# Low halves of 54 weight tiles by an adding DMA instead of VectorE, in a float32 decoder layer

## The chip, the cores and the metric

The kernel runs on one core of one Trainium2 chip. The metric is the device time of the whole program in microseconds, the median of several runs. A separate profiled execution gives the trace that is read here.

## The reference

One layer of a decoder trunk on 272 tokens (16 learned ones and 256 real), width 2048, all in float32: a half-step feed-forward network, a token mixer with two kinds of attention, and a second half-step feed-forward network. The change lies in the second half-step, which is computed for the 256 real tokens only:

```python
def _swiglu(x, w_gate, w_up, w_down):
    return (jax.nn.silu(x @ w_gate) * (x @ w_up)) @ w_down
...
h = h + FFN_RESIDUAL_WEIGHT * _swiglu(_rmsnorm(h, ffn2_norm[layer]), ffn2_w_gate[layer],
                                      ffn2_w_up[layer], ffn2_w_down[layer])
```

`w_gate` and `w_up` are 2048 x 5632, `w_down` is 5632 x 2048.

## The kernel before, in words

**Precision.** TensorE gets its factors as float32r. Each factor is split into a high part and a low part, and a product is three matmuls: high by high, high by low, low by high. For weights, ScalarE writes the high part `wh` (a copy from the float32 tile `raw` into a float32r tile), and VectorE then writes the low part `wl = raw - wh`.

**Units.** All weights go through TensorE in units of 512 KB (128 x 2 x 512), in the order of one list, `units`. For unit after unit the main loop calls `ahead(u)`, which loads (SP's DMA queue, into `raw`) and splits units that come later, and then `products(u)`. Loads run up to nine units ahead (`SECOND_AHEAD`), splits two (`SPLIT_AHEAD`). There are eight `raw` buffers in the second half-step, three of `wh` and three of `wl`. Inside each engine the instructions stay in the order that Tile's scheduler gives them; an engine that waits holds up all that stands behind it.

**The second half-step.** Its 11 column groups of 512 columns of gate and up are done in two ways. Nine (`SEVENS`) use a scheme of seven products instead of eight for each 2 x 2 block product: seven products `p1` to `p7`, each of four units with six matmuls, on sums and differences of weight blocks. The sums for p5, p6 and p7 were made in the first half-step and stored in DRAM (`sum`), p1 and p2 load parts of `w_gate`, p3 of `w_up`. p4 has no load: VectorE makes it in place from the raw tiles of p6 and p2. The order in a group is p1, p5, then p6, p2 and p4 by turns for each of the four units, then p3, p7. Between the units of the groups stand, one at a time, the plain units (12 matmuls each) of group 1 and of the down projection: one after each p2 unit, after every second unit of p5 and p3, and after the second unit of p1 and of p7. So a group is 28 units of six matmuls and ten plain ones.

In `split_unit` the copy of a group's unit is one line and its subtraction another (L1139 and L1145 in the profile; L1144 is the subtraction that makes p4). The plain units go through the helper `split` (L191 and L192). The matmuls of the groups are L1012, those of all other blocks L1213. Loads are issued at L1125 (groups) and L1130 (others). Evacuations of finished sums by ScalarE stand at L1019 (p1), L1022 (p5), L1033 (p4).

Other buffers: `slot` gives one of 25 buffers of 128 x 1024 float32 for values (tiles `v`), which also hold activations, sums and the evacuated results; `f` are the split activations.

Of the kernel before, what the change touches and what calls it, by code (L numbers as in the profile page):

```python
# [8 lines left out]
F32 = mybir.dt.float32  # L9
F32R = mybir.dt.float32r  # L10
AF = mybir.ActivationFunctionType
ALU = mybir.AluOpType
# [4 lines left out]
P = 128  # L17
# [15 lines left out]
SPLIT_BUFS = 3  # L33
LOAD_AHEAD = 6
SECOND_AHEAD = 9
SUMS_PACE = 0.94
SUMS_FROM = 20
PRE_BUFS = 9
# [14 lines left out]
def hybrid_layer(ctx: ExitStack, tc: tile.TileContext, x, meta_tokens, ffn1_norm, ffn1_w_gate, ffn1_w_up,  # L53
                 ffn1_w_down, mix_norm, w_in, b_forget, fox_q_norm, fox_k_norm, w_branch_fox, w_branch_sb,
                 w_out, ffn2_norm, ffn2_w_gate, ffn2_w_up, ffn2_w_down, out):
    nc = tc.nc
    act, dve, pe = nc.scalar, nc.vector, nc.tensor
# [13 lines left out]
    wp = ctx.enter_context(tc.tile_pool(name="weights", bufs=SPLIT_BUFS))  # L71
# [7 lines left out]
    def name(tag):  # L79
        uid[0] += 1  # L80
        return f"{tag}_{uid[0]}"

    def slot(shape, dt):
        return vp.tile(shape, dt, tag="v", name=name("v"))
# [105 lines left out]
    def split(hi, lo, src):  # L190
        act.activation(hi, src, AF.Copy)  # L191
        dve.tensor_tensor(lo, src, hi.bitcast(F32), op=ALU.subtract)  # L192
# [168 lines left out]
    def first_norm(c):  # L361

        ps = first_transposes(c)
        for i in range(2):
            first_parts(2 * c + i, ps[i])
        first_meta_parts(c)
        split_unit(c)
        first_residual(c, ps)
        for i in {1: (0, 1), 4: (4, 5), 5: (6,), 6: (7,), 7: ()}.get(c, (c,)):
            first_squares(i)  # L370
        if c == 2:
            meta_squares()
# [576 lines left out]
    def plain_group(g):  # L949

        u = {}
        factor = lambda i: norms["ffn2"].rtok[:, i:i + 1] if g == 0 else 1.0

        def ev_gate(i, ps):
            if i == 0:
                u["t"] = slot([P, 2, 512], F32)
            assert norms["ffn2"].done
            act.activation(u["t"][:, i, :], ps[:], AF.Silu, scale=factor(i))

        def ev_up(i, ps):  # L960
            s = u["t"][:, i, :]
            if g == 0:
                dve.scalar_tensor_tensor(s, ps[:], factor(i), s, op0=ALU.mult, op1=ALU.mult)
                free["g0"] = i == 1
            else:
                dve.tensor_tensor(s, ps[:], s, op=ALU.mult)
            if i == 1:
                lanes["turn"].append(turn(u["t"], hs2, 4 * g))

        def rhs(kt):  # L970
            if g == 0:
                return norms["ffn2"].rhs(kt)
            return [[forms[f"a{i + 1}{kt // 8 + 1}"][m][:, kt % 8, :] for i in range(2)] for m in range(2)]

        return [Block(w[0], 0, KT, g * 512, 512, rhs, NR, ev, True)
                for w, ev in ((ffn2_w_gate, ev_gate), (ffn2_w_up, ev_up))]
# [119 lines left out]
    def units_of(bs):  # L1096
        return [(b, k0, 1024 // b.cols) for b in bs for k0 in range(0, b.kts, 1024 // b.cols)]

    units = units_of(blocks)
# [5 lines left out]
    down = [down_blocks(t0, 4 * n, t0 + 4 * n == FT) for t0, n in zip(starts, PART)]  # L1105
    eight = [plain_group(1), *down]
    eight = [u for bs in eight for u in units_of(bs)]
    for g, p, u in seven:
        units.append((g, p, u))
        if p == "p2" or p in ("p5", "p3") and u % 2 or p in ("p1", "p7") and u == 1:  # L1110
            units.append(eight.pop(0))
    units += eight
    raws, halves, banks, newest = {}, {}, {}, []

    def raw_tile(shape):
        if loaded >= second and loaded % 8 >= RAW_BUFS:
            return ptile(shape, F32, "raw", 8 - RAW_BUFS)
        return wp.tile(shape, F32, tag="raw", name=name("raw"), bufs=RAW_BUFS)

    def load(u):  # L1120
        b, k0, n = units[u]
        if isinstance(b, Group):
            if k0 != "p4":
                t = raw_tile([P, 2, 512])
                nc.sync.dma_start(t[:], b.source(k0, n))  # L1125
                raws[u] = t
            return
        t = raw_tile([P, n, b.cols])
        rows = slice(b.row0 + k0 * P, b.row0 + (k0 + n) * P)
        q = nc.sync.dma_start(t[:], b.w[rows, b.col0:b.col0 + b.cols].rearrange("(k p) c -> p k c", p=P))  # L1130
        newest[:] = [q.ins]
        raws[u] = t

    def split_unit(u):
        b, k0, n = units[u]
        if isinstance(b, Group):
            wh, wl = (wp.tile([P, 2, 512], F32R, tag=t, name=name(t)) for t in ("wh", "wl"))
            raw = b.t.pop(k0) if k0 == "p4" else raws.pop(u)
            act.activation(wh[:], raw[:], AF.Copy)  # L1139
            if k0 == "p6":  # L1140
                b.t["p4"] = raw
            elif k0 == "p2":
                t = b.t["p4"]
                dve.tensor_tensor(t[:], t[:], raw[:], op=ALU.subtract)  # L1144
            dve.tensor_tensor(wl[:], raw[:], wh[:].bitcast(F32), op=ALU.subtract)  # L1145
            halves[u] = (wh, wl)
            return
        wh = wp.tile([P, n, b.cols], F32R, tag="wh", name=name("wh"))
        if b.stacked:
            raw, s = raws.pop(u), b.stacked  # L1150
            act.activation(wh[:], raw[:], AF.Copy)
            dve.tensor_tensor(wh[:, :, 32:32 + s], raw[:, :, :s], wh[:, :, :s].bitcast(F32), op=ALU.subtract)
            halves[u] = (wh, None)
            return
        wl = wp.tile([P, n, b.cols], F32R, tag="wl", name=name("wl"))
        split(wh[:], wl[:], raws.pop(u)[:])
        halves[u] = (wh, wl)
# [68 lines left out]
        if k0 + n == b.kts:  # L1226
            del banks[b]

    loaded = done = 0
    held = []  # L1230
    sums_due = 0.0

# [4 lines left out]
            yield 1  # L1237

    def ahead(u):
        nonlocal loaded, done, sums_due  # L1240
        if SUMS_FROM <= u < mixer - 2:
            sums_due += SUMS_PACE
            while sums_due >= 1:
                sums_due -= 1
                next(ahead_sums, None)
        while loaded < min(len(units), u + (LOAD_AHEAD if u < second else SECOND_AHEAD)):
            load(loaded)
            loaded += 1
        while done < min(len(units), u + 1 + SPLIT_AHEAD):
            split_unit(done)  # L1250
            done += 1
# [13 lines left out]
    for c in range(1, KT // 2):  # L1265
        with tc.issue_after(meta.ins):
            load_x(c)
            load(c)
    loaded = KT // 2
# [12 lines left out]
    done = KT // 2  # L1282
    start = KT // 2 - 1
    for u in range(start, len(units)):
        ahead(u)
        products(u)
# [33 lines left out]
```

## Time and profile before

| | |
|---|---|
| median of 3 runs | 2203.55 us (2202.67 to 2203.96) |
| profiled execution, its span | 2203.0 us, 34793 instructions |
| its own time outside the span | not listed apart; the span is 0.5 us under the median |
| granted TensorE clock, mean | 0.999 |
| DMA | 554.09 MB, mean 252 GB/s |
| GpSimd's DMA queue | 608 packets, 1.16 MB |

The profile names engines as PE (TensorE matmuls), PEld (its weight loads, which overlap), DVE (VectorE), ACT (ScalarE), POOL (GpSimd) and SP (the queue that issues most DMAs). `x<-y` says which tile is written from which. In square brackets, or after the bar, stands the idle time of the engine before an instruction and what ended it. The stage that the change touches lasts from about 1544 to 2148 us: nine groups.

### The profile page before, as it was taken

The numbers are of one execution on the slowest core, as the hardware profiler recorded it, in microseconds if no ns is written. First come the engines' busy times: TensorE is split into PE (matmuls) and PEld (weight loads), VectorE is DVE, ScalarE is ACT, GpSimd is POOL, SyncE is SP. The second block draws the span as 40 slices with busy tenths as digits, with TensorE's granted clock in tenths as the row PEclk, the third lists the DMA queues.
The fourth block names the chain that finished last, engine by engine and source line by source line (L and its number), as shares of the span: only waits on it lengthen the run. The fifth ranks groups of instructions, "written<-read, shape, count | busy, mean of one in ns | idle before, by whom it ended". The sixth has DMA issues, their size and how long they took to land.

```text
span 2203.0 us, 34793 instructions
## 1 busy us (share of the span) xinstructions
PE 2195.6 (100%) x13672; PEld 1992.5 (90%) x13672; DVE 1612.9 (73%) x1967; ACT 1174.5 (53%) x1475; POOL 52.5 (2%) x129
## 2 busy tenths in 40 slices
PE   9999999999999999999999999999999999999999
PEld 9999999999999999998899988888888888888887
DVE  6677666667766755889556776667888888888886
ACT  6344433334344454556435665458666666666663
POOL 0000000000000000110001100000000000000000
PEclk9999999999999999999999999999999999999999
DMA  7899999999999966555566556565788777888775
GB/s 226 275 335 330 334 319 345 338 347 334 341 339 339 327 201 191 168 162 164 183 191 171 145 153 200 182 188 164 240 269 271 263 257 263 273 273 268 261 256 173
DMA packets 262020, 554.09 MB, mean 252 GB/s; under 512 B 17288, under 2 KB 22240, under 8 KB 261856
## 3 DMA queue, kind: packets, MB, share of 16 engines
q1 hardware_dynamic: 259776, 548.34, 75.7%
q8 instruction: 107, 1.75, 0.3%
q10 hardware_dynamic: 1472, 2.37, 0.3%
q0 software_dynamic: 608, 1.16, 0.2%
q14 instruction: 57, 0.47, 0.1%
HBM read 493.07 MB, written 58.73 MB: 250 GB/s over the span
## 4 chain that ended last, share of the span: by engine, by line
PE 99%; DVE 0%; DMA 0%; ACT 0%; issue 0%; POOL 0%; SPq 0%; DVEq 0%; ACTq 0%; POOLq 0%
PE acc L1213 72%; PE acc L1012 16%; PE acc L1196 5%; PE acc L1199 3%; PE aux L729 1%; PE aux L602 1%; PE aux L442 1%; PE aux L700 0%; DMA v<-in_meta_tokens_dram 0%; PE aux L590 0%; PE acc L1174 0%; PE aux L875 0%; PE aux L340 0%; DVE wl L192 0%; PE aux L679 0%
## 5 line engine op out<-in xcount | busy, mean ns | idle before, releaser
L192 DVE TENSOR_TENSOR wl<-raw,wh 128x1024 fp32r<-128x1024 f32 (+1 forms) x609 | 743.7, 1222 | 420.4 <-ACT wh L191 416.7
L191 ACT ACTIVATE wh<-raw 128x1024 fp32r<-128x1024 f32 (+1 forms) x609 | 644.5, 1059 | 763.0 <-PE acc L1213 606.6
L1213 PE MATMUL acc<-v,wh 128*128 128x272 f32 x5264 | 991.6, 289 | 0.0
L1213 PEld LDWEIGHTS acc<-v,wh 128*128 128x128 f32 x5264 | 827.3, 189 | 0.4 <-ACT wh L191 0.2
L1213 PE MATMUL acc<-v,wl 128*128 128x272 f32 x2616 | 753.2, 289 | 0.6 <-DVE wl L192 0.6
L1213 PE MATMUL acc<-wh,v 128*128 128x512 f32 x1664 | 540.8, 392 | 0.0
L1213 PEld LDWEIGHTS acc<-v,wl 128*128 128x128 f32 x2616 | 490.8, 188 | 0.9 <-DVE wl L192 0.8
L1213 PEld LDWEIGHTS acc<-wh,v 128*128 128x128 f32 x1664 | 312.5, 188 | 64.4
L1145 DVE TENSOR_TENSOR wl<-raw,wh 128x1024 fp32r<-128x1024 f32 x252 | 305.1, 1222 | 41.6 <-ACT wh L1139 33.4
L1139 ACT ACTIVATE wh<-raw 128x1024 fp32r<-128x1024 f32 x252 | 266.5, 1060 | 124.1 <-PE acc L1213 74.0
L1213 PE MATMUL acc<-wl,v 128*128 128x512 f32 x832 | 327.8, 394 | 0.0
L1213 PEld LDWEIGHTS acc<-wl,v 128*128 128x128 f32 x832 | 156.2, 188 | 39.0 <-DVE wl L192 7.5
L1012 PE MATMUL acc<-wh,f 128*128 128x512 f32 x576 | 191.1, 393 | 0.0
L1196 PE MATMUL acc<-v,wh 128*128 128x512 f32 x512 | 160.5, 395 | 0.0
L1012 PE MATMUL acc<-wh,v 128*128 128x512 f32 x432 | 143.3, 389 | 0.0
L1012 PEld LDWEIGHTS acc<-wh,f 128*128 128x128 f32 x576 | 108.2, 188 | 22.5
L1199 PEld LDWEIGHTS acc<-v,wl 128*128 128x128 f32 x512 | 96.1, 188 | 21.9
L1012 PE MATMUL acc<-wl,f 128*128 128x512 f32 x288 | 113.2, 393 | 0.0
L1199 PE MATMUL acc<-v,wl 128*128 128x256 f32 x512 | 101.3, 279 | 0.0
L1012 PEld LDWEIGHTS acc<-wh,v 128*128 128x128 f32 x432 | 81.1, 188 | 16.9
L1012 PE MATMUL acc<-wl,v 128*128 128x512 f32 x216 | 84.0, 389 | 0.0
L1196 PEld LDWEIGHTS acc<-v,wh 128*128 128x128 f32 x512 | 78.4, 188 | 0.2
(267 smaller groups left out, 1392.6 us busy)
## 6 DMA issues: line engine op xcount, KB each, us to landing
raw<-in_ffn_w_down_dram SPq DMA_DIRECT2D x176, 512.0 KB, 5.4
raw<-in_ffn_w_gate_dram SPq DMA_DIRECT2D x175, 512.0 KB, 5.3
raw<-in_w_in_dram SPq DMA_DIRECT2D x162, 512.0 KB, 3.7
raw<-in_ffn_w_up_dram SPq DMA_DIRECT2D x140, 512.0 KB, 5.1
sum<-pre SPq DMA_DIRECT2D x108, 512.0 KB, 6.6
raw<-sum SPq DMA_DIRECT2D x108, 512.0 KB, 4.7
pre<-in_ffn_w_up_dram SPq DMA_DIRECT2D x72, 512.0 KB, 6.7
pre<-in_ffn_w_gate_dram SPq DMA_DIRECT2D x36, 512.0 KB, 6.9
```

The costliest lines, as they stand in the source:

```text
L191: act.activation(hi, src, AF.Copy)
L192: dve.tensor_tensor(lo, src, hi.bitcast(F32), op=ALU.subtract)
L442: pe.transpose(p[:, (2 * j + i) * P:(2 * j + i + 1) * P], u[:, i, c:c + P], ident[:])
L602: pe.matmul(po[:, :NR], a[:, ks], b[:, i * NR:(i + 1) * NR], start=n == 0, stop=n == 6)
L729: pe.matmul(o, a, b, start=start, stop=stop, skip_group_check=True)
L1012: pe.matmul(ps[:], a[:, kt, :], b[:, i, :], start=fresh and kt == 0 and m == 0, stop=kt == 7 and m == 2, skip_group_check=True)
L1139: act.activation(wh[:], raw[:], AF.Copy)
L1145: dve.tensor_tensor(wl[:], raw[:], wh[:].bitcast(F32), op=ALU.subtract)
L1196: pe.matmul(ps[:].rearrange("p (a t) -> p a t", a=2), wh[:, i, cs], x[:, :, :NR], start=k0 + i == 0, stop=False, skip_group_check=True)
L1199: pe.matmul(ps[:, :NR], wl[:, i, cs], x[:, 0, :NR], start=False, stop=k0 + i == b.kts - 1, skip_group_check=True)
L1213: pe.matmul(o, a, c, start=first and m == 0, stop=last and m == len(terms) - 1)
```

## The change

For the four p2 units of every group, and for the plain units behind the second unit of p1 and of p7 (six units in each of nine groups, 54 in all, the set `summed`), VectorE's subtraction is left out. In its place a new step `seed(u)`, up to five units ahead (`SEED_AHEAD`), takes a value buffer (`slot`), has ScalarE write the negated high part into it (a copy with scale -1 from `raw`), and has GpSimd issue a DMA that adds the same 512 KB of weights from DRAM to it. That tile is then the low part. The high part is copied from `raw` as before. So each of the 54 units is fetched from DRAM twice.

```diff
+SEED_AHEAD = 5
...
+    summed = set()
     for g, p, u in seven:
+        if p == "p2":
+            summed.add(len(units))
         units.append((g, p, u))
         if p == "p2" or p in ("p5", "p3") and u % 2 or p in ("p1", "p7") and u == 1:
+            if p in ("p1", "p7"):
+                summed.add(len(units))
             units.append(eight.pop(0))
...
+    def source_of(u):
+        b, k0, n = units[u]
+        if isinstance(b, Group):
+            return b.source(k0, n)
+        rows = slice(b.row0 + k0 * P, b.row0 + (k0 + n) * P)
+        return b.w[rows, b.col0:b.col0 + b.cols].rearrange("(k p) c -> p k c", p=P)
...
+    lows = {}
+
+    def seed(u):
+
+        t = slot([P, 2, 512], F32R)
+        act.activation(t[:], raws[u][:], AF.Copy, scale=-1.0)
+        nc.gpsimd.dma_start(t[:], source_of(u), accum_op=ALU.add)
+        lows[u] = t
...
-            wh, wl = (wp.tile([P, 2, 512], F32R, tag=t, name=name(t)) for t in ("wh", "wl"))
+            wh = wp.tile([P, 2, 512], F32R, tag="wh", name=name("wh"))
+            wl = lows.pop(u) if u in lows else wp.tile([P, 2, 512], F32R, tag="wl", name=name("wl"))
...
-            dve.tensor_tensor(wl[:], raw[:], wh[:].bitcast(F32), op=ALU.subtract)
+            if u not in summed:
+                dve.tensor_tensor(wl[:], raw[:], wh[:].bitcast(F32), op=ALU.subtract)
...
+        if u in lows:
+            act.activation(wh[:], raws.pop(u)[:], AF.Copy)
+            halves[u] = (wh, lows.pop(u))
+            return
...
+        while seeded < min(len(units), u + 1 + SEED_AHEAD):
+            if seeded in summed:
+                seed(seeded)
+            seeded += 1
         while done < min(len(units), u + 1 + SPLIT_AHEAD):
             split_unit(done)
             done += 1
```

ScalarE's list before, in group 5 (about 1764 to 1780 us), from the end of p1 through p5 to the first p2 unit. L191 writes plain units and transposed results (`v`), L1139 the groups' units; `wh_2915` is the high part of the first p2 unit, from `raw_2893`.

```order
L1139 ACTIVATE wh_2894_18613<-raw_2872_18520 128x1024
L1019 ACTIVATE v_2896_18623<-acc_2881_18554 128x512
L191 ACTIVATE v_2899_18631<-aux_2898_18626 128x2x256
L191 ACTIVATE wh_2901_18636<-raw_2875_18532 128x1024
L1139 ACTIVATE wh_2904_18647<-raw_2878_18548 128x1024
L1139 ACTIVATE wh_2907_18659<-raw_2882_18561 128x1024
L191 ACTIVATE wh_2910_18677<-raw_2885_18573 128x1024
L1139 ACTIVATE wh_2913_18689<-raw_2890_18599 128x1024
L1022 ACTIVATE v_2897_18624<-acc_2903_18640 128x512
L1139 ACTIVATE wh_2915_18700<-raw_2893_18611 128x1024
L191 ACTIVATE wh_2918_18719<-raw_2900_18634 128x1024
```

The same place of ScalarE's list after (L1139 is now L1161, the other lines are one further down); L1151 is the negated copy.

```order
L1161 ACTIVATE wh_2894_18632<-raw_2873_18541 128x1024
L1020 ACTIVATE v_2896_18642<-acc_2881_18573 128x512
L192 ACTIVATE v_2899_18650<-aux_2898_18645 128x2x256
L192 ACTIVATE wh_2901_18655<-raw_2876_18553 128x1024
L1161 ACTIVATE wh_2904_18666<-raw_2879_18569 128x1024
L1151 ACTIVATE v_2907_18678<-raw_2893_18630 128x1024
L1161 ACTIVATE wh_2908_18681<-raw_2882_18580 128x1024
L192 ACTIVATE wh_2911_18699<-raw_2885_18592 128x1024
L1161 ACTIVATE wh_2914_18711<-raw_2890_18618 128x1024
L1023 ACTIVATE v_2897_18643<-acc_2903_18659 128x512
L1161 ACTIVATE wh_2916_18722<-raw_2893_18630 128x1024
L1151 ACTIVATE v_2918_18739<-raw_2910_18697 128x1024
```

The negated copy of the first p2 unit (`raw_2893`) comes five rows ahead of its ordinary copy; the other rows keep their order.

GpSimd's list had nothing after the memset at the stage's start; now the 54 transfers follow it, these the first (`v` is the tile of the negated high part):

```order
L829 MEMSET shift_15166 128x48
L1152 DMA v_16806<-in_ffn_w_gate_dram 128x2x512
L1152 DMA v_16989<-in_ffn_w_gate_dram 128x2x512
L1152 DMA v_17050<-in_ffn_w_gate_dram 128x2x512
L1152 DMA v_17106<-in_ffn_w_gate_dram 128x2x512
L1152 DMA v_17160<-in_ffn_w_gate_dram 128x2x512
L1152 DMA v_17319<-in_ffn_w_up_dram 128x2x512
```

They stand in the order of the negated copies, one behind the other in GpSimd's queue. VectorE's list has 1954 rows before and 1900 after; SP's has 1053 in both.

More of the change, by code (lines that the diff above doesn't have):

```diff
@@ L1124, in load @@
                 t = raw_tile([P, 2, 512])
-                nc.sync.dma_start(t[:], b.source(k0, n))
+                nc.sync.dma_start(t[:], source_of(u))
                 raws[u] = t
@@ L1128, in load @@
         t = raw_tile([P, n, b.cols])
-        rows = slice(b.row0 + k0 * P, b.row0 + (k0 + n) * P)
-        q = nc.sync.dma_start(t[:], b.w[rows, b.col0:b.col0 + b.cols].rearrange("(k p) c -> p k c", p=P))
+        q = nc.sync.dma_start(t[:], source_of(u))
         newest[:] = [q.ins]
         raws[u] = t
+    lows = {}
[4 more added lines that the diff above has]
+        lows[u] = t
     def split_unit(u):
@@ L1227, in products @@
             del banks[b]
-    loaded = done = 0
+    loaded = seeded = done = 0
     held = []
@@ L1239, in ahead @@
     def ahead(u):
-        nonlocal loaded, done, sums_due
+        nonlocal loaded, seeded, done, sums_due
         if SUMS_FROM <= u < mixer - 2:
```

## The prediction

> **What bounds the kernel now.** I read the parts of the page on busy time and on the chain first, then cut the span into stages, then read the waits of TensorE, and the DMA last.
>
> ```profile
> PE 2195.6 (100%) x13672; PEld 1992.5 (90%) x13672; DVE 1612.9 (73%) x1967; ACT 1174.5 (53%) x1475; POOL 52.5 (2%) x129
> PE 99%; DVE 0%; DMA 0%; ACT 0%; issue 0%; POOL 0%; SPq 0%; DVEq 0%; ACTq 0%; POOLq 0%
> ```
>
> TensorE is busy for the whole span and 99% of the chain that ended last. So work taken off VectorE pays only where TensorE stands waiting for VectorE, and a new transfer costs only where TensorE comes to wait for it. All 54 changed units lie in the stage of the seven-product groups, which the view by windows cuts out (columns: window, its length, busy us and count of PE, PEld, DVE, ACT, POOL, then granted clock, DMA share, GB/s). The first half-step stands beside it, as the stage with the busiest DMA.
>
> ```profile
> 50.00:811.00 761.00, 760.43 (x6056) 760.17 (x6055) 509.88 (x587) 305.93 (x363) 5.50 (x18) 1.00 0.94 324
> 1544.00:2148.00 604.00, 604.00 (x2672) 491.12 (x2672) 518.93 (x493) 397.36 (x421) 0.00 (x0) 1.00 0.80 263
> ```
>
> In the 604 us VectorE is busy for 519 (86%), ScalarE for 397 (66%), GpSimd for nothing, and the 16 DMA engines for 0.80. What TensorE waits for there, from the view of waits of its weight loads from 1500 us on:
>
> ```profile
> PEld acc L1213 <- DVE wl L192: 9.1, 30, 0.4
> PEld acc L1012 <- DVE wl L1145: 1.3, 7, 0.2
> ```
>
> 37 waits, 10.4 us. Two kinds of them, from the timeline of the weight loads:
>
> ```profile
> 1761.32 0.19 PEld L1213 LDWEIGHTS acc<-wl,v 128*128 128x128 f32 x1 [0.18 <-DVE wl L192]
> 1770.18 0.19 PEld L1213 LDWEIGHTS acc<-wl,v 128*128 128x128 f32 x1 [0.40 <-DVE wl L192]
> ```
>
> And what they cost, from the chain in order of time (start, us, what):
>
> ```profile
> 1617.47 2.72 PE acc L1213 x12
> ...
> 1634.92 2.99 PE acc L1213 x12
> ```
>
> A plain unit of 12 matmuls takes 2.72 us, and 2.99 where the long wait (0.37 to 0.40) falls. The long wait stands in the plain units after p5 and p3, which the change leaves as they are; the one of 0.18 in the plain unit after p1, which it changes.
>
> **The change part by part.** The work that moves, from the groups by line of the 604 us (busy us, mean ns of one, idle before):
>
> ```profile
> L1145 DVE TENSOR_TENSOR wl<-raw,wh 128x1024 fp32r<-128x1024 f32 x248 | 300.2, 1222 | 41.2 <-ACT wh L1139 33.4
> L1139 ACT ACTIVATE wh<-raw 128x1024 fp32r<-128x1024 f32 x249 | 263.4, 1060 | 123.2 <-PE acc L1213 74.0 <-PE acc L1012 40.5 <-issue 6.7
> ```
>
> The nearest issue of GpSimd's, from the view of its source line (ns, least, median, most):
>
> ```profile
> L626 POOL DMA_DIRECT2D nck<-negc x8: 543/546/566, 849.0 to 1005.3; - x8
> ```
>
> VectorE loses 54 subtractions of 1.222 us, 66 us, and falls to 453 of 604. On the path that is worth the short waits in the changed units: eight of 0.18 after p1 and at most the seven of L1145, 2.7 us in all if each counted in full, and nothing where the 2.72 already holds them. I take 0. The long waits stay, because ScalarE is late there and not VectorE (its timeline, and one row of VectorE's):
>
> ```profile
> 1766.83 0.60 ACT L1019 ACTIVATE v<-acc 128x512 f32<-128x512 f32 x1 [0.28 <-PE acc L1012]
> 1767.32 0.59 ACT L191 ACTIVATE v<-aux 128x512 fp32r<-128x512 f32 x1
> 1767.80 1.06 ACT L191 ACTIVATE wh<-raw 128x1024 fp32r<-128x1024 f32 x1
> 1768.75 1.06 ACT L1139 ACTIVATE wh<-raw 128x1024 fp32r<-128x1024 f32 x1
> 1770.01 1.06 ACT L1139 ACTIVATE wh<-raw 128x1024 fp32r<-128x1024 f32 x1 [0.20 <-PE acc L1012]
> 1773.00 1.06 ACT L191 ACTIVATE wh<-raw 128x1024 fp32r<-128x1024 f32 x1 [1.93 <-PE acc L1213]
> ...
> 1776.22 1.05 ACT L1139 ACTIVATE wh<-raw 128x1024 fp32r<-128x1024 f32 x1
> ...
> 1768.90 1.22 DVE L192 TENSOR_TENSOR wl<-raw,wh 128x1024 fp32r<-128x1024 f32 x1 [0.26 <-ACT wh L191]
> ```
>
> VectorE stood idle for 0.26 us for the copy of 1767.80, which stood behind two evacuations that TensorE had just released; their order is unchanged.
>
> ScalarE gains 54 negated copies. Their form has no row; the copy of the same shape takes 1.060 us, so 57 us, and 455 of 604 (75%). At the place above the negated copy of the first p2 unit stands between the rows of 1768.75 and 1770.01. It runs from 1769.81 (the end of the former) to 1770.87 and moves the next copy by 0.86 us. The idle 1.93 us ahead of 1773.00 takes that up: cost 0. Behind a negated copy stand the ordinary copies and the evacuations in ScalarE's queue, and it waits for its weights to have landed, earlier than the ordinary copy did (SP's timeline, and the loads of the 604 us with their median time to landing):
>
> ```profile
> 1764.16 0.38 SPq L1125 DMA_DIRECT2D raw<-in_ffn_w_gate_dram  x1
> ...
> raw<-sum SPq DMA_DIRECT2D x108, 512.0 KB, 4.7
> raw<-in_ffn_w_down_dram SPq DMA_DIRECT2D x76, 512.0 KB, 5.0
> raw<-in_ffn_w_gate_dram SPq DMA_DIRECT2D x75, 512.0 KB, 5.1
> raw<-in_ffn_w_up_dram SPq DMA_DIRECT2D x44, 512.0 KB, 4.6
> ```
>
> This p2 unit was issued at 1764.16 and lands 5.1 us later, at 1769.3: 0.5 us before ScalarE comes to it. Before, its copy was the one at 1776.22, 7 us after the landing. So a lead of 7 us shrinks to about half a microsecond: no cost while loads land in 5 us, and a stall of ScalarE as soon as they take 6.
>
> GpSimd's queue is empty in this stage; 54 issues of about 0.55 us (the nearest row, for a quarter of the bytes) block nobody. SP's queue keeps its 1053 rows; the seeded plain units give their buffer back a subtraction earlier, which only starts loads earlier.
>
> The transfers are what remains. 263 GB/s over 604 us are 159 MB, the 303 loads of 512 KB above; 0.80 of 604 is 483 us of all 16 engines, so 1.595 us for each load, with 121 us free. The added transfer of 512 KB has no row. Its lower bound is one load, 54 x 1.595 = 86 us, which fits (569 of 604, 0.94). But its result is the tile's content plus the weights, so two operands of 512 KB come in for the 512 KB that go out, where a load has one in and one out. At twice a load it is 172 us, 51 us more than is free; as three transfers (a load, a fetch of the tile and a write) 258 us, 137 too many. I take twice, by its two operands. Once the engines are the bound, the stage lasts 655 us. The 7 us by which loads ran ahead are used up once, so the sum is 2203.0 + 51 - 7 = 2247 us, against the profiled execution's own span of 2203.0, 0.5 us under the median of the runs, 2203.55. For this case alone: if the engines move bytes as in the first half-step (324 / 0.94 = 345 GB/s), 215.5 MB take 625 us and the sum is 2217; if they cannot be kept busier than the 0.94 seen there, 655 / 0.94 = 697 and 2296.
>
> A rule of the Trainium skill bears on this price: its page "Collectives: The Full Stack", section "The bandwidth ceiling: the fold count and why AG ≠ RS ≠ AR", says that an adding transfer is slower for its two source reads and not for the addition, 62.28 against 32.35 GB/s, a factor of 1.93. By that the sum would be 2241; no run here shows it yet.
>
> What is late next, if so: the low half of a seeded unit at TensorE, or the loads at ScalarE, both behind full DMA engines.
>
> **Rivals.** *The transfer is hidden (same).* It costs one load, the share rises to 0.94, which the first half-step bears with TensorE busy for 760.4 of 761 us. It must also land in time. At the place above it can start at 1770.87, and TensorE loads that low half here:
>
> ```profile
> 1779.61 0.19 PEld L1012 LDWEIGHTS acc<-wl,f 128*128 128x128 f32 x1
> ```
>
> 8.7 us. The nearest landings are from 880 to 1100 us, where GpSimd also issues, and, for loads at a share of 0.94, from 50 to 811 us (the third row):
>
> ```profile
> raw<-in_w_in_dram SPq DMA_DIRECT2D x54, 512.0 KB, 3.7
> ...
> nck<-negc POOLq DMA_DIRECT2D x6, 136.0 KB, 3.8
> ...
> raw<-in_ffn_w_down_dram SPq DMA_DIRECT2D x88, 512.0 KB, 5.8
> ```
>
> Taking off the movement (1.6 and 0.4 us) leaves 2.1 and 3.4, so GpSimd's way costs 1.3 us more: 5.1 + 1.3 = 6.4 us, and 5.8 + 1.3 = 7.1 at 0.94, under 8.7. Time 2203, at most 2206. The Trainium skill's page "DMA: Bandwidth & Descriptors", section "Anatomy of one DMA — SWDGE (gpsimd) path", has 2.0 us plus the bytes at 436 GB/s, 3.2 us here, and so would side with this rival; the trace disagrees, since the 136 KB took 3.8 us where the rule has 2.3.
>
> *Hidden in bytes, late in time (slower).* The engines hold out, but a landing passes 8.7 us, or loads pass the 0.5 us that ScalarE has left, as the 5.8 just would. Each 0.7 us late at 54 places is 38 us, and about half, as the next transfer is under way meanwhile: 2222.
>
> *Three transfers.* 2203 + 137 - 7 = 2333.
>
> *VectorE's relief pays (faster).* If all 37 waits of TensorE went with VectorE's lower load, 10.4 us: 2193. It decides for faster once 4.4 us of them go; against it stands that ScalarE, not VectorE, ends the long ones.
>
> That the subtractions stay is no rival: VectorE's list is 54 rows shorter.
>
> **How the numbers follow.** Twice a load 0.48 (2217 to 2296), hidden 0.24, late in time 0.12, three transfers 0.10, relief 0.06. I predict the likeliest, 2247. The range from 2201 to 2300 leaves out the relief and the three transfers, 0.16. Within 0.2% (4.4 us) is about what a measurement of this kernel can tell from no change: faster 0.06, same 0.24, slower 0.70.
>
> **What would show it.** Right: in the stage a DMA share near 1.0, the new transfers landing after 9 us or more, loads after 6 or more, TensorE's weight loads waiting for the transfers or ScalarE's negated copies for raw tiles, and the stage longer than 604 us by 40 to 50. Wrong: a share of about 0.94 and landings of 6 to 7 us; then the second operand costs the engines nothing and the time stays. A stage longer at a share well below 1 would mean that landing time, not bytes, decides.

## The result, and the profile after

The changed kernel takes 2258.98 us in the median (2255.01 to 2260.18) against 2203.69 for the kernel before on the same chip: a ratio of 1.0249 (95% interval 1.0237 to 1.0262), 55 us slower. Its profiled execution has a span of 2256.9 us. The two lines of its page on busy time and on the chain:

```profile
PE 2212.7 (98%) x13672; PEld 1990.1 (88%) x13672; DVE 1550.2 (69%) x1913; ACT 1219.7 (54%) x1529; POOL 119.2 (5%) x183
PE 70%; issue 25%; DMA 2%; POOL 2%; DVE 1%; ACT 0%; POOLq 0%; SPq 0%; DVEq 0%; ACTq 0%
```

VectorE has its 63 us less and ScalarE its 45 us more in the whole span, but TensorE is no longer the whole chain. (The 25% of "issue" is time for which the profile shows no releaser; the waits below tell more.) The view by windows, same columns as before, shows where the time went:

```profile
1544.00:2201.00 657.00, 620.83 (x2664) 489.41 (x2663) 454.86 (x438) 442.06 (x474) 65.11 (x54) 0.99 0.94 284
2201.00:2257.00 56.00, 51.13 (x228) 41.59 (x227) 36.66 (x44) 21.47 (x22) 0.00 (x0) 1.00 0.53 174
```

The stage of the groups takes 657 us instead of 604 for the same matmuls (2664 and 2672 in the records), what follows it 56 instead of 55. So the loss is all in the stage. The DMA share is 0.94, not 1. The waits of TensorE's weight loads there (us in total, times, longest):

```profile
PEld acc L1240 <- DVE wl L193: 16.9, 31, 1.1
PEld acc L1013 <- DMA v<-in_ffn_w_gate_dram: 14.6, 14, 2.2
PEld acc L1013 <- DVE wl L1168: 13.3, 15, 1.1
PEld acc L1013 <- ACT wh L1161: 7.4, 10, 1.9
PEld acc L1240 <- DMA v<-in_ffn_w_down_dram: 7.0, 6, 1.9
PEld acc L1240 <- ACT wh L192: 6.7, 6, 1.6
```

With two rows of 1.0 us that is 68 us, where the kernel before had 10. There are two kinds. Some 24 us are waits for the adding transfers (`v<-`). The other 44 are waits for ScalarE's high parts and for VectorE's low parts. What holds ScalarE up, from its own waits:

```profile
ACT v L1151 <- DMA raw<-in_ffn_w_gate_dram: 28.7, 17, 3.7
ACT v L1151 <- DMA raw<-in_ffn_w_down_dram: 25.2, 11, 4.0
```

The negated copies (L1151) wait 57 us in all for raw tiles that have not landed; in the kernel before ScalarE waited for no load in this stage. The timeline shows one such wait going through to TensorE (issue of a load, three rows of ScalarE, a weight load of TensorE):

```profile
1803.47 0.37 SPq L1138 DMA_DIRECT2D raw<-in_ffn_w_gate_dram  x1
...
1805.60 1.06 ACT L1161 ACTIVATE wh<-raw 128x1024 fp32r<-128x1024 f32 x1 [0.34 <-PE acc L1013]
1809.97 1.06 ACT L1151 ACTIVATE v<-raw 128x1024 fp32r<-128x1024 f32 x1 [3.31 <-DMA raw<-in_ffn_w_gate_dram]
1810.94 1.04 ACT L1161 ACTIVATE wh<-raw 128x1024 fp32r<-128x1024 f32 x1
...
1812.03 0.19 PEld L1013 LDWEIGHTS acc<-wh,f 128*128 128x128 f32 x1 [1.47 <-ACT wh L1161]
```

ScalarE starts on the tile of a load issued at 1803.47 only 6.5 us later. It stands idle for 3.31 us in front of the negated copy of that tile, the next high part comes late, and TensorE waits 1.47 us for it. The DMA rows of the stage (queue: packets, MB, share of 16 engines; then count, size, median us to landing):

```profile
q1 hardware_dynamic: 68363, 158.44, 68.8%
q0 software_dynamic: 14416, 27.79, 24.6%
...
raw<-sum SPq DMA_DIRECT2D x107, 512.0 KB, 5.4
...
raw<-in_ffn_w_gate_dram SPq DMA_DIRECT2D x75, 512.0 KB, 6.4
...
v<-in_ffn_w_gate_dram POOLq DMA_DIRECT2D x37, 512.0 KB, 8.9
v<-in_ffn_w_down_dram POOLq DMA_DIRECT2D x15, 512.0 KB, 8.4
```

By their MB there are 302 loads and 53 recorded transfers of 512 KB. 68.8% of 657 us is 452, 1.50 us of all 16 engines for a load; 24.6% is 162, 3.05 for an adding transfer: twice a load. Loads land in 5.4 to 6.6 us (4.6 to 5.1 before), the two larger groups of transfers in 8.4 and 8.9.

The profile leaves three theories open. *Bytes:* the engines cannot carry loads and transfers in 604 us. *Late:* the transfers land after TensorE needs them. *Held:* ScalarE, whose queue is in order, is held up by loads that the negated copies ask for early. The experiments take them apart. In the first expectations SCALARE stands for a cost of the 54 extra copies on ScalarE itself; HELD comes in with the later ones.

### The profile page after: what moved, and what is told of

Same layout as the page of the kernel before. It is cut to its first block, busy times and chain, and to the rows that moved or that the text cites. A ratio compares the mean times of both kernels' runs of the same rounds, so it can differ in the third digit from the quotient of the medians.

```text
span 2256.9 us, 34969 instructions
## 1 busy us (share of the span) xinstructions
PE 2212.7 (98%) x13672; PEld 1990.1 (88%) x13672; DVE 1550.2 (69%) x1913; ACT 1219.7 (54%) x1529; POOL 119.2 (5%) x183
## 4 chain that ended last, share of the span: by engine, by line
PE 70%; issue 25%; DMA 2%; POOL 2%; DVE 1%; ACT 0%; POOLq 0%; SPq 0%; DVEq 0%; ACTq 0%
PE acc L1240 58%; PE acc L1223 5%; PE acc L1226 3%; POOL v L1152 2%; DMA v<-in_ffn_w_down_dram 1%; PE acc L1013 1%; PE aux L730 1%; PE aux L603 1%; DMA v<-in_ffn_w_gate_dram 0%; DMA raw<-in_ffn_w_gate_dram 0%; DVE wl L193 0%; PE aux L443 0%; PE aux L701 0%; PE aux L591 0%; DMA v<-in_meta_tokens_dram 0%
## 5 line engine op out<-in xcount | busy, mean ns | idle before, releaser
L193 DVE TENSOR_TENSOR wl<-raw,wh 128x1024 fp32r<-128x1024 f32 (+1 forms) x591 | 722.1, 1223 | 474.7 <-ACT wh L192 472.9
L192 ACT ACTIVATE wh<-raw 128x1024 fp32r<-128x1024 f32 (+1 forms) x591 | 625.1, 1058 | 717.5 <-PE acc L1240 586.7
L1240 PEld LDWEIGHTS acc<-v,wh 128*128 128x128 f32 x5264 | 827.4, 189 | 0.4 <-ACT wh L192 0.2
L1168 DVE TENSOR_TENSOR wl<-raw,wh 128x1024 fp32r<-128x1024 f32 x216 | 260.3, 1222 | 102.8 <-ACT wh L1161 99.3
L1161 ACT ACTIVATE wh<-raw 128x1024 fp32r<-128x1024 f32 x252 | 262.7, 1055 | 106.3 <-PE acc L1013 41.4
L1240 PE MATMUL acc<-wl,v 128*128 128x512 f32 x766 | 303.4, 396 | 5.2 <-DVE wl L193 5.2
L1240 PEld LDWEIGHTS acc<-wl,v 128*128 128x128 f32 x766 | 144.5, 189 | 43.0 <-DVE wl L193 14.5
L1013 PE MATMUL acc<-wl,v 128*128 128x512 f32 x216 | 85.5, 396 | 6.7 <-DVE wl L1168 6.6
L1151 ACT ACTIVATE v<-raw 128x1024 fp32r<-128x1024 f32 x54 | 56.8, 1056 | 57.4 <-DMA raw<-in_ffn_w_gate_dram 28.7
L1013 PE MATMUL acc<-wl,f 128*128 128x512 f32 x216 | 84.4, 391 | 1.4 <-DVE wl L1168 1.4
```

The costliest lines, as they stand in the source:

```text
L1013: pe.matmul(ps[:], a[:, kt, :], b[:, i, :], start=fresh and kt == 0 and m == 0, stop=kt == 7 and m == 2, skip_group_check=True)
L1151: act.activation(t[:], raws[u][:], AF.Copy, scale=-1.0)
L1240: pe.matmul(o, a, c, start=first and m == 0, stop=last and m == len(terms) - 1)
```

## The experiments

All times are medians beside the kernel before on the same chip. For orientation, all of them in one table, with sums from the profiled executions: the DMA share from 1544 to 2148 us, all waits of TensorE's weight loads from 1544 us on, those of them for the transfers, and ScalarE's waits for raw tiles. In plain_copy, no_transfer, near_source, high_source, high_ahead7 and high_none the low parts hold other values than the product needs; these kernels serve for their times alone.

| kernel | us | over before | DMA share | TensorE's waits | of them for transfers | ScalarE's for raw |
|---|---|---|---|---|---|---|
| before | 2203.7 | | 0.80 | 10 | | 0 |
| high_none | 2206.1 | +2 | 0.80 | 13 | | 0 |
| high_ahead7 | 2206.7 | +3 | 0.99 | 14 | 1 | 3 |
| high_unread | 2208.9 | +6 | 0.99 | 17 | | 0 |
| no_transfer | 2212.5 | +8 | 0.79 | 18 | | 21 |
| only18 | 2227.5 | +23 | 0.83 | 36 | 9 | 33 |
| plain_copy | 2227.7 | +24 | 0.90 | 40 | 1 | 40 |
| high_source | 2247.6 | +44 | 0.94 | 55 | 45 | 0 |
| raw9 | 2253.0 | +50 | 0.94 | 59 | 23 | 62 |
| after | 2259.0 | +55 | 0.94 | 70 | 25 | 57 |
| near_source | 2267.5 | +64 | 0.92 | 67 | 12 | 59 |
| ahead3 | 2269.6 | +66 | 0.92 | 75 | 28 | 63 |
| unread | 2272.3 | +68 | 0.93 | 67 | | 68 |
| near_unread | 2274.2 | +71 | 0.91 | 75 | | 72 |

**1. One operand instead of two (plain_copy).**

```diff
-        nc.gpsimd.dma_start(t[:], source_of(u), accum_op=ALU.add)
+        nc.gpsimd.dma_start(t[:], source_of(u))
```

> The 54 transfers overwrite the tile instead of adding to it (the low part is then the weights themselves; the negated copies, queues and waits stay as in the changed kernel), so one operand comes in where two did. Theory BYTES (the second operand costs the DMA engines as much as a load, demand 452+162 us and more): a transfer takes about 1.5 us of 16 engines instead of 2.99, the stage's DMA share falls to about 0.90 or the stage gets shorter at the same share, loads land in about 5 to 6 us, time 2203 to 2215. Theory LATE (the way through GpSimd's queue and its landing time of 8.9 us cost the time, not the engines): the landing falls by 1.5 us at most, time 2235 to 2255. Theory SCALARE (54 more copies on ScalarE cost it): unchanged, 2255 to 2260.

2227.69 us, ratio 1.0103 (1.0088 to 1.0118). The DMA rows, from 1544 to 2195 us:

```profile
q1 hardware_dynamic: 71660, 164.80, 74.6%
q0 software_dynamic: 14688, 28.32, 15.0%
...
v<-in_ffn_w_gate_dram POOLq DMA_DIRECT2D x37, 512.0 KB, 6.0
```

15.0% of 651 us over 54 transfers is 1.81 us each, against 3.05 with the addition; landing falls from 8.9 to 6.0 us. TensorE waits for hardly any transfer (1 us), yet 24 us are lost at a share of 0.90. None of the three expectations fits alone: the engines are not full, and TensorE does not wait for the transfers, but ScalarE still waits 40 us for raw tiles.

**2. No transfer at all (no_transfer).**

```diff
-        nc.gpsimd.dma_start(t[:], source_of(u), accum_op=ALU.add)
```

> The negated copies stay, the 54 transfers are left out altogether (the low part is then minus the high part; nothing is fetched twice), VectorE's subtractions stay left out. All that is left of the change is 57 us more on ScalarE and 66 us less on VectorE. Theories BYTES and LATE: 2203 to 2206, TensorE's waits in the stage near the 10 us of the kernel before. Theory SCALARE: 2230 to 2260. Theory RELIEF (VectorE's lower load would pay if nothing else were in the way): 2193 to 2199.

2212.45 us, 1.0036 (1.0022 to 1.0051), between the expectations. The share is that of the kernel before, and still 8 us are lost. ScalarE's waits:

```profile
ACT v L1151 <- DMA raw<-in_ffn_w_down_dram: 13.8, 12, 3.0
ACT v L1151 <- DMA raw<-in_ffn_w_gate_dram: 6.0, 13, 0.8
```

Even with loads landing as fast as before, some negated copies come before their tile. ScalarE's list is the same row for row here, in plain_copy and in the changed kernel; its waits for raw tiles are 21, 40 and 57 us, and the loads from `w_gate` land in 5.0, 5.7 and 6.4 us. So the transfers cost time in this way by making the loads land later. No gain from VectorE's relief shows.

**3. Transfers that nobody reads (unread).** VectorE subtracts all low parts again, TensorE reads those; seeds and transfers are made.

```diff
-            wl = lows.pop(u) if u in lows else wp.tile([P, 2, 512], F32R, tag="wl", name=name("wl"))
+            wl = wp.tile([P, 2, 512], F32R, tag="wl", name=name("wl"))
+            lows.pop(u, None)
...
-            if u not in summed:
+            if True:
...
-        if u in lows:
-            act.activation(wh[:], raws.pop(u)[:], AF.Copy)
-            halves[u] = (wh, lows.pop(u))
-            return
+        lows.pop(u, None)
```

> Negated copies and adding transfers are all made, but VectorE subtracts as in the kernel before and TensorE reads that low part: nobody waits for what the 54 transfers bring, apart from the reuse of their buffers. Theory BYTES: the engines carry the same load, so loads are late and ScalarE waits for them, time 2240 to 2258, share 0.93 to 0.95. Theory LATE (TensorE waits for the landing of the low tiles): 2203 to 2215. A time halfway, near 2230, would mean that the loss is made of both about equally, as TensorE's new waits behind transfers (25 us) and behind ScalarE and VectorE (the rest) suggest.

2272.26 us, 1.0321 (1.0298 to 1.0345): slower than the change itself, though no wait for a transfer can be left. TensorE's waits:

```profile
PEld acc L1013 <- ACT wh L1162: 21.5, 13, 3.1
PEld acc L1013 <- DVE wl L1169: 19.7, 22, 1.6
PEld acc L1238 <- ACT wh L192: 13.5, 6, 4.2
PEld acc L1238 <- DVE wl L193: 12.2, 31, 1.1
```

They are all behind ScalarE, which waits 68 us for raw tiles, or behind VectorE, which works on ScalarE's results. So the late landings at TensorE are not the only route. Bytes or Held remain.

**4. Only the 18 plain units (only18).**

```diff
-        if p == "p2":
-            summed.add(len(units))
```

> Only the 18 plain units (behind the second unit of p1 and of p7) get their low part by an adding transfer, the 36 p2 units are subtracted by VectorE as before. Theory BYTES: 18 x 2.99 = 54 us on top of the 483 us of the 303 loads, 537 of 604 us, a share of 0.89, below what the stage bore: 2203 to 2208. Theory LATE: the loss goes by the number of transfers, 18 of 54 of the 55 us: 2218 to 2225. Theory SCALARE: the same third, 2218 to 2225.

2227.46 us, 1.0107 (1.0092 to 1.0122), just above the 2218 to 2225 that LATE and SCALARE expected. The window of the stage:

```profile
1544.00:2148.00 604.00, 588.90 (x2581) 473.09 (x2580) 481.07 (x459) 398.11 (x423) 20.50 (x17) 1.00 0.83 270
```

A third of the transfers at a share of 0.83, with engine time left over, lose 42% of the whole. That speaks against Bytes.

**5. and 6. The negated copy from another raw tile (near_source), and that with unread tiles (near_unread).**

```diff
-        act.activation(t[:], raws[u][:], AF.Copy, scale=-1.0)
+        act.activation(t[:], raws[min(raws)][:], AF.Copy, scale=-1.0)
```

> The negated copy reads the raw tile that is split next instead of the one five units ahead (so the low parts hold wrong values; the DMA still adds the weights of the right unit). ScalarE's work, the 54 adding transfers, their queue and TensorE's reading of them stay; the only thing gone is that ScalarE stands still behind a load that has not landed (57 us of it in the changed kernel). Theory HELD (the loss comes through ScalarE, held up by loads that the negated copy asks for too early): its waits for raw fall under 5 us, time 2203 to 2222. Theory BYTES (the engines cannot carry 452 + 162 = 614 us in 604): share stays at 0.94 to 0.97 and loads stay late, 2240 to 2258. Theory LATE (landing at TensorE): no change in its waits for the tiles, 25 us, time 2225 to 2235.

> As the run before, and besides VectorE subtracts all low parts as in the kernel before and TensorE reads those: nobody waits for a seeded tile, and ScalarE does not wait for early loads. What is left of the change is the 54 adding transfers on the DMA engines and 57 us of ScalarE. Theory HELD: 2203 to 2215. Theory BYTES: 2240 to 2260. Against the run before it gives what TensorE's waits for the tiles cost: theory LATE puts this run at 2203 to 2210 and the one before 20 or more above it.

2267.47 us (1.0287, 1.026 to 1.0315) and 2274.19 (1.0322, 1.0307 to 1.0337). They lie even above what Bytes expected, but the edit did not do what it was for. ScalarE's waits in near_source:

```profile
ACT v L1151 <- DMA raw<-in_ffn_w_down_dram: 33.8, 16, 3.9
ACT v L1151 <- DMA raw<-sum: 14.7, 7, 3.5
```

With two smaller rows 59 us, where the changed kernel has 57. The scheduler moved 32 of the 54 copies forward in ScalarE's list, by 1 to 9 rows, now that their tile was an earlier one, and there they stood in front of loads again. These two runs tell nothing of the theories, save that the place on ScalarE is the scheduler's choice.

**7. Seeds three units ahead (ahead3).**

```diff
-SEED_AHEAD = 5
+SEED_AHEAD = 3
```

> Seeds go three units ahead instead of five: the negated copy comes about two units (3.4 us) later, so loads have that much more time, and the adding transfer has that much less until TensorE wants the tile (about 5.3 us where it lands in 7 to 9). Theory HELD: ScalarE's waits for raw fall under 10 us, but TensorE then waits 2 to 3 us for most of the 54 tiles, partly covered by each other: 2250 to 2300, its waits now put down to the transfers and not to ScalarE. Theory BYTES: the same demand, 2250 to 2260, waits split as before.

2269.63 us, 1.0295 (1.0278 to 1.0313). ScalarE's waits for raw tiles stayed at 63 us, since the constant hardly moved anything: in ScalarE's list 53 of the 54 negated copies stand in the same row as in the changed kernel. The first one moved five rows back, to two rows ahead of its unit's ordinary copy, and TensorE's longest wait for a transfer became 7.0 us. The run tells nothing of the trade between the two leads.

**8. and 9. The negated copy from a tile that needs no load (high_source), and that with unread tiles (high_unread).** The copy now reads the high part that ScalarE has just written, so it cannot come to stand in front of a load. Against the changed kernel 22 of the 54 copies stand one to four rows later in ScalarE's list, and none earlier.

```diff
-        act.activation(t[:], raws[u][:], AF.Copy, scale=-1.0)
+        act.activation(t[:], halves[done - 1][0][:].bitcast(F32), AF.Copy, scale=-1.0)
```

> The negated copy reads the high part that ScalarE has just written for another unit, so it stands in the same place of ScalarE's list as in the changed kernel (within a row or two) but waits for no load at all (the low parts hold wrong values; ScalarE's work, the 54 adding transfers and TensorE's reading of them stay). This is what near_source was meant to be; there the scheduler moved the copies forward until they waited for loads again (59 us). Theory HELD (the loss is ScalarE standing in its queue behind loads that have not landed): waits for raw under 5 us, time 2203 to 2222. Theory BYTES (614 us of transfers do not fit into 604 us, nor more than a share of 0.94): 2240 to 2260, with the waits for raw tiles now at the high parts' copies. Theory LATE (landing of the low tiles at TensorE): waits for v tiles of 25 us stay and are most of what is left, 2225 to 2235.

> The same, and VectorE subtracts all low parts as in the kernel before and TensorE reads those. What is left of the change is 57 us of ScalarE and the 54 adding transfers' load on the DMA engines, with nobody waiting for them. Theory HELD: 2203 to 2212. Theory BYTES: 2240 to 2270. Theory LATE: 2203 to 2210 here, and the run before 20 us above it.

2247.62 us (1.0205, 1.0188 to 1.0223) and 2208.92 (1.0024, 1.0015 to 1.0033). The stage of high_unread, and its two large queues in these 604 us:

```profile
1544.00:2148.00 604.00, 603.02 (x2651) 486.35 (x2650) 512.82 (x488) 444.28 (x471) 63.84 (x53) 1.00 0.99 307
```

```profile
q1 hardware_dynamic: 67969, 157.18, 73.1%
q0 software_dynamic: 14416, 27.79, 25.8%
```

The loads of the kernel before in its 604 us:

```profile
q1 hardware_dynamic: 68459, 158.59, 79.7%
```

This settles Bytes. The engines carry 300 loads and 53 adding transfers in 604 us, at a share of 0.99, while TensorE is busy for 603 of them. 441 us go to the loads, 1.47 each (481 us before, 1.59 each), and 156 to the transfers, 2.94 each. With nobody waiting for either, the full traffic and ScalarE's 57 us cost 6 us. Between unread (+68) and high_unread (+6) only the source of the negated copy differs, with it the place of some copies in the list, and ScalarE's 68 us of waits for raw tiles are gone: theory Held is shown as one route. The other route is in TensorE's waits in high_source:

```profile
PEld acc L1013 <- DMA v<-in_ffn_w_gate_dram: 23.5, 24, 2.2
PEld acc L1240 <- DMA v<-in_ffn_w_down_dram: 17.1, 15, 1.9
PEld acc L1240 <- DVE wl L193: 10.6, 30, 0.4
```

With two smaller rows there are 42 waits for transfers, 45 us, 1.06 us each, and the waits behind ScalarE are gone. Between high_source (+44) and high_unread (+6) TensorE's reading of the transferred tiles and VectorE's share of the work differ: theory Late. Held alone had put high_source at 2203 to 2222, and Late at 2225 to 2235; both were too low. The time lies in the range of Bytes, 2240 to 2260, but not for its reason: Bytes had put high_unread at 2240 or more.

**10. Nine raw buffers (raw9).**

```diff
-SECOND_AHEAD = 9
-V_BUFS = 25
+SECOND_AHEAD = 10
+V_BUFS = 24
...
-        if loaded >= second and loaded % 8 >= RAW_BUFS:
-            return ptile(shape, F32, "raw", 8 - RAW_BUFS)
+        if loaded >= second and loaded % 9 >= RAW_BUFS:
+            return ptile(shape, F32, "raw", 9 - RAW_BUFS)
```

> The changed kernel whole, with nine raw buffers instead of eight in the second half-step and loads ten units ahead, paid for with one of the 25 value buffers: each load may start about one unit (1.7 us) earlier. Theory HELD: the 30 negated copies that wait 1.9 us on average mostly find their tile, ScalarE's waits for raw fall from 57 us to 15 to 30, time 2215 to 2235. Theory BYTES: full engines give the earlier start back as a longer landing; waits for raw and the time stay, 2250 to 2258, and the median landing of loads rises from 6.3 to about 8 us.

2252.98 us, 1.0226 (1.0211 to 1.0241): 6 us better than the change, with intervals that overlap, and ScalarE's waits for raw tiles stay (62 us). The time is what Bytes expected, but the landing of loads did not rise to 8 us (6.0 to 6.3). Nor did the copies get their lead: in ScalarE's list 27 of the 54 moved forward, by 1 to 9 rows, as in near_source. What one more buffer gives with the copies in their place stays open. A kernel with ten raw buffers and 23 value buffers (raw10) came to a deadlock and gave no time.

**11. The transfer two units earlier (high_ahead7).** On top of high_source:

```diff
-SEED_AHEAD = 5
+SEED_AHEAD = 7
```

> As high_source (the negated copy reads a high part just written and waits for no load; the low parts hold wrong values), but the seed goes seven units ahead instead of five, so GpSimd issues each adding transfer about two units (3.4 us) earlier; TensorE reads the tiles as before. Theory LATE (with the loads' wait out of the way, what is left of high_source's 39 us is that the transfer lands after 9 us, about 1 us past its need): TensorE's waits for the transfers fall from 45 us to under 5, time 2203 to 2215. Theory BYTES in its last form (TensorE reading tiles that full engines are still writing costs by itself): 2235 to 2250.

2206.73 us, 1.0014 (1.0005 to 1.0023). The stage, and TensorE's waits there:

```profile
1544.00:2148.00 604.00, 601.47 (x2657) 488.28 (x2655) 456.03 (x437) 443.26 (x473) 63.84 (x53) 1.00 0.99 308
```

```profile
PEld acc L1013 <- ACT wh L1161: 5.8, 9, 0.7
PEld acc L1240 <- DVE wl L193: 4.4, 12, 0.5
PEld acc L1240 <- ACT wh L192: 2.5, 9, 0.3
PEld acc L1240 <- DMA v<-in_ffn_w_down_dram: 1.2, 2, 0.9
```

In ScalarE's list 45 of the 54 copies stand one to three rows earlier than in high_source. TensorE reads all 54 tiles, the share is 0.99, the transfers still land in about 9 us (8.8 to 9.6), and the loss is gone. So the second route was lead and nothing else: at TensorE the transfers were 1 us late, and two units earlier they are in time.

**12. ScalarE's copies alone (high_none).** high_source without the transfer line.

> As high_source, but without the 54 transfers (the low part is then a negated high part of another unit). What is left of the change is 57 us more on ScalarE, none of it in front of a load, and 66 us less on VectorE. Theory RELIEF (VectorE's lower load pays once nothing hides it): 2193 to 2199, TensorE's waits for VectorE under 5 us. Against it: ScalarE ends those waits, 2202 to 2206, the waits for VectorE's subtractions near the 10 us of the kernel before.

2206.10 us, 1.0011 (1.0002 to 1.0020). TensorE's waits for VectorE:

```profile
PEld acc L1239 <- DVE wl L193: 13.3, 38, 0.4
```

13.3 us where the kernel before has 9.1: with 54 subtractions less on VectorE they have not shrunk. The relief pays nothing: VectorE itself now waits 149 us for ScalarE's high parts, against 81 before.

No version beat the kernel before, and these last two show why none was to be expected: with both waits taken away the time comes back to that of the kernel before, not below it.

## Why the prediction was right in its number and wrong in its reason

The predicted 2247 us lies 12 below the measured 2259, and the direction was right. That the numbers are so close is luck: the 51 us of the sum were engine time that was not needed, and the 55 us measured came through waits for which the sum had nothing. Step by step:

- **The price of an adding transfer.** Twice a load was forecast, 3.05 to 1.50 us was measured (2.94 to 1.47 in high_unread). Not all of that is the second operand: without the addition GpSimd's transfer took 1.81, beside loads of 1.55 (plain_copy, 74.6% of 651 us for 314 loads). The Trainium skill's page "Collectives: The Full Stack", section "The bandwidth ceiling: the fold count and why AG ≠ RS ≠ AR", has a factor of 1.93 between a ring's AllGather and its ReduceScatter, and puts it down to the two source reads of an addition. The trace is near it against a load (2.0), but not against the same transfer without the addition (3.05 to 1.81, 1.69).
- **The engines as the bound: the step that failed.** The sum took 0.80 of 604 us, 483 us, as the need of the 303 loads, 1.595 us each, whatever else runs. Beside the transfers a load took 1.47 to 1.50 us, so the whole need was 441 + 156 = 597 us instead of 655, and it fitted into 604. (All 303 loads and 54 transfers at these prices come to 604, so nothing was to spare.) "51 us more than is free" does not exist; high_unread and high_ahead7 show the stage at a share of 0.99 with at most 6 us lost. What the sum had at nothing, TensorE's waits, grew by 60 us. The case of its own at 345 GB/s was nearer to this, and it too made the bytes the bound. (Its other case, 2296, leaves out the 7 us that the sum takes off, and should be 2289. No run shows these 7 us by themselves.)
- **The rival that came true** is "hidden in bytes, late in time", given 0.12 and 2222 us. It named both routes: a landing past 8.7 us, and loads past the 0.5 us that ScalarE has left. Its size was wrong. GpSimd's way was to land in 6.4 to 7.1 us, and its two larger groups landed in 8.4 and 8.9 (that estimate took its base from loads, and the extra operand as no time). For the transfers alone high_source shows +44, for ScalarE alone unread shows +68. The 55 of the change are less than the sum of both; that one wait covers the other would explain it, and so would the clock in part (below), but neither is shown to be all of it.
- **ScalarE at cost 0.** Half right. The 57 us of copies do cost next to nothing (high_none, +2). But the step said "no cost while loads land in 5 us", and no_transfer, with loads at 4.6 to 5.0 us, lost 8 us with 21 us of waits: the 0.5 us of lead was read at one place, and other places had less. Its warning of "a stall of ScalarE as soon as they take 6" came true (6.2 to 6.6 us for loads from the weights), but the sum had no term for it.
- **VectorE's relief at 0.** Right (high_none, no_transfer).
- **GpSimd's issue.** 1.2 us each (65.11 us for 54 in the stage) instead of 0.55. In high_ahead7 it costs nothing.
- **The test that it set itself.** A share near 1.0 was to show it right; "a stage longer at a share well below 1 would mean that landing time, not bytes, decides". The stage was longer by 53 us at 0.94, which the experiments bear out as the second case.
- **The landing time by rule.** The Trainium skill's page "DMA: Bandwidth & Descriptors", section "Anatomy of one DMA — SWDGE (gpsimd) path", has 2.0 us and the bytes at 436 GB/s, an estimate of 3.2 us here. The trace disagrees for transfers among other traffic: without the addition they landed in 5.2 to 6.0 us at a share of 0.90 (plain_copy), with it in 7.0 to 8.5 at 0.83 (only18), and in 8.4 and 8.9 for the two larger groups at 0.94.

Unread loses 13 us more than the change itself, though TensorE waits no longer there (67 us against 70). The trace has the clock for it: in the stage the granted clock is 0.50 for 34 us, in stretches of 3.4 or 6.8 us, and for 7 us in the changed kernel. At half the clock the 27 us more cost up to 14. What stays open is why ScalarE waits longer for raw tiles in unread, 68 us against 57. VectorE holds each raw tile longer there, which would start loads later, but no run takes that apart.

The ledger of the table closes without bytes: what TensorE's waits grew by is what the time grew by, within 6 us, in ten of the thirteen kernels. In after 70 - 10 = 60 for 55 us, in high_source 45 for 44, in raw9 49 for 50. The three others, near_source, unread and near_unread, lose 6 to 11 us more than their waits, and in these the granted clock of the stage was 0.97.

## What to carry to other kernels

A DMA share below 1 times the time is not the need of the transfers: the same loads took 8% less of the engines when these were full, so free engine time is a bad measure of what still fits, and a share well under 1 no proof that nothing is late: traffic that fits still made the loads land later. When work moves from an engine to a transfer, count the two leads, of its input before the engine that prepares it and of its result before the engine that reads it; an in-order engine that asks 2 us too early stops everything behind it. And look where the scheduler has put the moved instruction before reading a test of lead: a constant that says "ahead" may change nothing.

## What the runs showed of the hardware that was not expected

- A load of 512 KB took 1.59 us of all 16 engines at a share of 0.80 (481 us by the queue's 79.7% of 604, for 158.59 MB), and 1.47 at 0.99.
- A GpSimd transfer of 512 KB into a float32r tile took 1.81 us of the engines without the addition and 3.05 with it; GpSimd was busy for 0.71 us per issue (38.56 us for 54) without and 1.2 with it.
- In three kernels in which TensorE waited for 67 to 75 us the granted clock of the stage fell to 0.97, while ahead3 with as many waits kept 0.99. The clock is not a little lower throughout: in unread it is 0.50 from 1586.3 to 1592.9 us and 1.00 from 1594 to 1626. No run shows what sets such a stretch off; in raw9 TensorE stood idle for 3.2 us at 2052 without one.
